# A hybrid decoder step: the four strip products of a group of cached pages placed side by side in TensorE's queue

## Chip, cores and metric

The kernel runs on one core of a Trainium2 chip. The metric is the device time of one launch in microseconds, as the median of several runs. The trace is of one execution of the same program.

## The reference

One decoder layer is computed for a prompt of 1024 tokens and for 8 sample tokens, each of which has 4096 cached positions in 32 pages of 128. What matters here is the attention of the sample tokens over their pages:

```python
past_k = cache_k[l][page_table].reshape(dec_batch, -1, 2 * DA_HEADS, DA_HEAD_DIM)
past_v = cache_v[l][page_table].reshape(dec_batch, -1, DA_HEADS, DA_VDIM)
...
s = jnp.einsum('bqnd,bknd->bnqk', qf, k.astype(jnp.float32)) * DA_SCALE
scores.append(jnp.where(rel >= 0, s - slopes * rel, NEG_INF))
...
p = jax.nn.softmax(jnp.concatenate(scores, axis=-1), axis=-1)
p = p.reshape(B, DA_HEADS, 2, Lq, p.shape[-1])
a = p[:, :, 0] - lam * p[:, :, 1]
outs.append(jnp.einsum('bhqk,bkhv->bqhv', a[..., start:start + n], v.astype(jnp.float32)))
```

Around it stand, for the prompt and the sample tokens alike, a gated feed-forward network (1024 to 2816 and back), one input projection, a linear recurrence with four heads, the attention with four heads of two maps each, one output projection, and a second feed-forward network.

## The kernel before, in words

**The main stream** is the dense work: the feed-forward networks (L382 for the gate and up products, L441 for the down products), the input projection (L508) and the output projection (L382 again). Every product is done in three parts with operands split into a high and a low half (`wH`, `wL`, `xn`, `h`). Weights come as 256 KB tiles `wr` by a DMA that SyncE issues (L360); ScalarE makes `wH` of them and VectorE or GpSimd `wL` (L110).

**Side streams** are woven into it. One does the recurrence and the attention of the prompt (L666 to L862). The other, the sample stream, goes through the pages of the 8 sample tokens. For token b it loads the 32 key pages into tiles `kv` (L984), multiplies each by the query on GpSimd (L1014) and sums on VectorE into the scores `sS` (L1015). After token b's last key page come its softmax (L1023 to L1049) and then, while the key pages of token b+1 pass, its value pages. Key and value pages share 8 buffers `kv`.

**The value pages are taken in groups of four** (`VP = 4`), 64 groups in all. When the fourth page of a group has been asked for, four *strip products* (L1065) multiply the group's 32 columns of weights (128 x 32) with the four pages (128 x 512), one page each, into rows 0 to 31, 32 to 63, 64 to 95 and 96 to 127 of one PSUM tile `mx`: strip j stands in columns 32j to 32j+31 of the array. VectorE then adds the tile to `sacc` (L1069, or L1067 for the first group of a token). There are 256 strip products; the trace shows each as two MATMUL records (two passes over the same 512 columns), so 512 records. `mx` has two buffers, which the recurrence (L690, L691) and the attention's scores (L821) use as well.

**What sets the order**: the program is written out in one order, and a list scheduler with a timeline of its own gives each engine its queue. An instruction's rank is its place in the written order, less an offset where a block is marked: `hp(n)` moves what is in it up by n instructions, and `tc.issue_after(x)` holds what is in it until x has been placed. Most evacuations of the main stream stand in `hp()` (6000), the prompt's side stream in `hp(3000)`, the sample stream in none. Each engine then works through its queue in order, and waits on semaphores.

Of the kernel before, what the change touches and what calls it, by code (L numbers as in the profile page):

```python
# [63 lines left out]
def kernel(ctx: ExitStack, tc: tile.TileContext, I, O):  # L64
    nc = tc.nc
    ACT, DVE, POOL, PE, SP = nc.scalar, nc.vector, nc.gpsimd, nc.tensor, nc.sync
# [12 lines left out]
    def ST(tag, shape, dt=F32, bufs=1):  # L79
        return samp.tile(shape, dt, name=tag, tag=tag, bufs=bufs)  # L80
# [7 lines left out]
    def MX():  # L88
        return psum.tile([P, 512], F32, name="mx", tag="mx", bufs=2)
# [10 lines left out]
    def hp(n=6000):  # L100
        return tc.high_priority(offset=n)
# [875 lines left out]
    def page(name, src, i):  # L977
        t = kv()
        if i % 4 == 0:

            with tc.issue_after(issued[-4].ins) if len(issued) >= 4 else nullcontext():
                _, numbers[name] = nc.values_load_multi_w_load_instructions(pages[0:1, i:i + 4], engines=[SP.engine], min_val=0, max_val=NPOOL - 1,
                                                                             skip_runtime_bounds_check_because="the page table holds numbers of pages")
        issued.append(SP.dma_start(t, src[bass.ds(numbers[name][i % 4], 1)].rearrange("o t c -> (o t) c")))  # L984
        return t

    def sample_attention():
# [65 lines left out]
        vts = {}  # L1053

        def values(b, i):
            Sb = S[b][0]
            vts[i % VP] = page("v", cv, b * NPG + i)
            if i % VP < VP - 1:
                return
            if i == VP - 1:  # L1060
                S["acc"] = ST("sacc", [P, 512], bufs=1)
            po = MX()
            w = Sb.rearrange("p i n -> p (i n)")[:, 8 * (i - VP + 1):8 * (i + 1)]
            for j in range(VP):
                PE.matmul(po[32 * j:32 * j + 32, :], w, vts[j], start=True, stop=True, tile_position=(0, 32 * j))  # L1065
            if i == VP - 1:
                DVE.tensor_copy(S["acc"], po)  # L1067
            else:
                DVE.tensor_tensor(out=S["acc"], in0=po, in1=S["acc"], op=ALU.add)  # L1069

        VP = 4
# [7 lines left out]
        for b in range(NB + 1):  # L1079
            if b < NB:  # L1080
                begin(b)
            for i in range(NPG):
                if b < NB:
                    keys(b, i)
                    yield 1.2
                if b > 0:
                    values(b - 1, i)
                    yield 1.2
            if b > 0:
                end(b - 1)  # L1090
            if b < NB:
                softmax(b)
# [240 lines left out]
```

## Time and profile before

| what | value |
|---|---|
| median of 3 runs | 2511.26 us (2506.85 to 2513.51) |
| the profiled execution | 2503.05 us |
| its span, first to last instruction | 2501.2 us |
| TensorE busy in the span | 2433.6 us (97%) |
| VectorE, ScalarE, GpSimd busy | 1592.6, 924.7, 797.9 us |

The profiled execution's own time lies 1.85 us above its span and 8.21 us below the median of the runs. "Busy" counts the time in which an engine executes at least one instruction; matmuls overlap, so their starts, not their durations, tell what one costs.

### The profile page before, as it was taken

Reading aid. Unit: us, or ns where it says so; the run is one execution under the profiler, and the core shown is the slowest. Engines: PE = TensorE matmul, PEld = TensorE weight load, DVE = VectorE, ACT = ScalarE, POOL = GpSimd, SP = SyncE. Lnnn points to the kernel's source line nnn. Section 1 sums busy time; section 2 is a strip of 40 time slices with the busy share of each in tenths; the row PEclk is TensorE's granted clock in tenths of the full one; section 3 lists DMA queues with packets and bytes.
Section 4 is the critical chain, followed back from the end, with each engine's and each line's share of the span. In section 5 each row is a group of like instructions: output and inputs, shape, how many; then the busy total and the mean of one; then the engine's idle time right before and its main releaser. Section 6 shows DMA issues by size and latency. Waiting matters only on the chain.

```text
span 2501.2 us, 44071 instructions
## 1 busy us (share of the span) xinstructions
PE 2433.6 (97%) x15613; PEld 2071.6 (83%) x15613; DVE 1592.6 (64%) x3326; ACT 924.7 (37%) x1921; POOL 797.9 (32%) x660
## 2 busy tenths in 40 slices
PE   7999999989999999999999999999999999999999
PEld 6999999979867766777778866767677879999999
DVE  6555656595687655757548678776675765655554
ACT  4332334435433322434444433323344544322222
POOL 4100001380243434544435454554452220000000
PEclk9999999999999999999999999999999999999999
DMA  4333334684465647667666775566676743233332
GB/s 135 91 92 93 100 93 119 199 287 128 136 198 165 191 152 214 214 194 237 195 202 187 229 241 156 178 203 188 209 226 189 203 141 117 89 91 92 94 94 73
DMA packets 273534, 402.35 MB, mean 161 GB/s; under 512 B 29785, under 2 KB 104794, under 8 KB 273314
## 3 DMA queue, kind: packets, MB, share of 16 engines
q1 hardware_dynamic: 273314, 399.54, 52.4%
q8 instruction: 123, 2.02, 0.3%
q14 instruction: 97, 0.79, 0.1%
HBM read 361.23 MB, written 38.21 MB: 160 GB/s over the span
## 4 chain that ended last, share of the span: by engine, by line
PE 64%; DVE 6%; DMA 4%; POOL 2%; issue 1%; ACT 1%; SPq 1%; POOLq 0%; DVEq 0%; ACTq 0%
PE mm L382 31%; PE mm L441 13%; PE mm L508 6%; PE mx L1065 6%; DMA kv<-in_cache_k 2%; PE my L723 1%; PE mx L821 1%; POOL kv L1014 1%; PE my L851 1%; DMA xt<-ot 1%; DVE sS L1015 1%; DVE wL L110 1%; PE mx L690 0%; PE my L844 0%; PE mx L691 0%
## 5 line engine op out<-in xcount | busy, mean ns | idle before, releaser
L382 PE MATMUL mm<-xn,wH 128*128 128x256 f32 (+2 forms) x4800 | 1110.5, 324 | 6.0 <-DVE ft L482 2.5
L382 PEld LDWEIGHTS mm<-xn,wH 128*128 128x128 f32 x4800 | 795.4, 190 | 113.4 <-issue 42.8
L382 PE MATMUL mm<-xn,wL 128*128 128x256 f32 (+2 forms) x2400 | 777.0, 324 | 0.0
L110 ACT CAST wH<-wr 128x512 fp32r<-128x512 f32 x672 | 413.6, 619 | 826.8 <-PE mm L382 433.0
L110 DVE TENSOR_TENSOR wL<-wr,wH 128x512 fp32r<-128x512 f32 x504 | 410.5, 816 | 195.1 <-ACT wH L110 157.0
L382 PEld LDWEIGHTS mm<-xn,wL 128*128 128x128 f32 x2400 | 454.6, 189 | 55.0 <-issue 19.3
L441 PE MATMUL mm<-h,wH 128*128 128x264 f32 (+2 forms) x2112 | 489.1, 324 | 5.6 <-DVE tiny L701 2.8
L1014 POOL TENSOR_TENSOR kv<-kv,ss 128x512 f32<-128x512 f32 x256 | 357.9, 1404 | 426.8 <-DMA kv<-in_cache_k 299.1
L441 PEld LDWEIGHTS mm<-h,wH 128*128 128x128 f32 x2112 | 348.3, 189 | 58.5 <-issue 21.8
L441 PE MATMUL mm<-h,wL 128*128 128x264 f32 (+2 forms) x1056 | 340.4, 322 | 0.0
L508 PE MATMUL mm<-wH,xn 128*128 128x256 f32 (+1 forms) x1728 | 325.9, 288 | 7.7 <-DVE ft L482 3.9
L110 POOL TENSOR_TENSOR wL<-wr,wH 128x512 fp32r<-128x512 f32 x168 | 228.5, 1361 | 270.2 <-ACT wH L110 224.1
L421 POOL TENSOR_TENSOR ft<-ft,acc 128x256 f32<-128x256 f32 (+1 forms) x110 | 101.8, 926 | 666.1 <-DVE ft L419 663.5
L508 PEld LDWEIGHTS mm<-wH,xn 128*128 128x128 f32 (+1 forms) x1728 | 260.1, 181 | 28.6 <-issue 14.2
L1015 DVE TENSOR_REDUCE sS<-kv 128x8 f32<-128x512 f32 x256 | 172.4, 679 | 137.5 <-POOL kv L1014 137.1
L508 PE MATMUL mm<-wL,xn 128*128 128x256 f32 (+1 forms) x864 | 248.0, 287 | 1.3 <-POOL wL L110 0.9
L441 PEld LDWEIGHTS mm<-h,wL 128*128 128x128 f32 x1056 | 199.3, 189 | 21.3 <-issue 7.5
L443 DVE SCALAR_TENSOR_TENSOR xr<-mm,xr 128x264 f32<-128x264 f32 (+2 forms) x288 | 146.2, 512 | 104.9 <-PE mm L441 104.3
L1065 PE MATMUL mx<-kv,sS 128*32 128x512 f32 x512 | 165.4, 604 | 0.2 <-DVE sS L1049 0.2
L508 PEld LDWEIGHTS mm<-wL,xn 128*128 128x128 f32 (+1 forms) x864 | 156.1, 181 | 9.6 <-issue 5.0
L419 DVE TENSOR_TENSOR ft<-ft,mm 128x256 f32<-128x256 f32 (+2 forms) x132 | 67.2, 509 | 77.5 <-PE mm L382 77.2
L110 ACT CAST h<-ft 128x256 fp32r<-128x256 f32 (+2 forms) x132 | 63.1, 478 | 92.6 <-POOL ft L421 76.5
(219 smaller groups left out, 2299.2 us busy)
## 6 DMA issues: line engine op xcount, KB each, us to landing
kv<-in_cache_k SPq DMA_DIRECT2D x256, 256.0 KB
kv<-in_cache_v SPq DMA_DIRECT2D x256, 256.0 KB
wr<-in_ffn_w_gate SPq DMA_DIRECT2D x176, 256.0 KB
wr<-in_ffn_w_up SPq DMA_DIRECT2D x176, 256.0 KB
wr<-in_ffn_w_down SPq DMA_DIRECT2D x176, 256.0 KB
wr<-in_w_in SPq DMA_DIRECT2D x96, 256.0 KB
aq<-qt SPq DMA_DIRECT2D x64, 128.0 KB
wr<-in_w_out SPq DMA_DIRECT2D x32, 256.0 KB
```

Source lines behind the costliest of these rows:

```text
L110: return ACT.copy(H, src), (eng or DVE).tensor_tensor(out=L, in0=src, in1=H.bitcast(F32), op=ALU.subtract)
L382: newest[0] = PE.matmul(ps[:, :w], a, b[k][:, :w], start=k == 0 and j == 0, stop=k == n - 1 and j == 2)
L419: DVE.tensor_tensor(out=t, in0=t, in1=pu[:, :sl.w], op=ALU.mult)
L421: POOL.tensor_tensor(out=t, in0=t, in1=sl.acc, op=ALU.mult)
L441: newest[0] = PE.matmul(ps[:, :w], a[:, cs], b[:, :w], start=j == 0 and q == 0, stop=j == m - 1 and q == 2)
L443: DVE.scalar_tensor_tensor(out=sl.xr[d][:, :w], in0=ps[:, :w], scalar=0.25, in1=sl.xr[d][:, :w], op0=ALU.mult, op1=ALU.add)
L508: newest[0] = PE.matmul(ps[:tb, 0:256], a, b, start=k == 0 and j == 0, stop=k == KC - 1 and j == 2)
L723: PE.matmul(pa[:, i * 64:i * 64 + 64], XL[:, i], right(XR[:, i], l0 + i), start=True, stop=True)
L821: PE.matmul(ps[:, :m], qx[:, j, x], KT[:, j, pc * 512:pc * 512 + m], start=x == 0, stop=x == 1)
L1014: POOL.tensor_tensor(out=kt, in0=kt, in1=qb, op=ALU.mult)
L1015: DVE.tensor_reduce(out=Sb[:, i], in_=kt.rearrange("p (n d) -> p n d", d=64), op=ALU.add, axis=AX.X)
L1065: PE.matmul(po[32 * j:32 * j + 32, :], w, vts[j], start=True, stop=True, tile_position=(0, 32 * j))
```

## The change

The four strip products of a group are written so that the newest page's comes first, in a block that is moved up by 5000, and the other three are held until it has been placed.

```diff
             po = MX()
             w = Sb.rearrange("p i n -> p (i n)")[:, 8 * (i - VP + 1):8 * (i + 1)]
-            for j in range(VP):
-                PE.matmul(po[32 * j:32 * j + 32, :], w, vts[j], start=True, stop=True, tile_position=(0, 32 * j))
+
+            def strip(j):
+                return PE.matmul(po[32 * j:32 * j + 32, :], w, vts[j], start=True, stop=True, tile_position=(0, 32 * j))
+
+
+            with hp(5000):
+                m = strip(VP - 1)
+                with tc.issue_after(m.ins):
+                    for j in range(VP - 1):
+                        strip(j)
             if i == VP - 1:
                 DVE.tensor_copy(S["acc"], po)
```

In TensorE's queue of before, the 256 strip products stand in 156 pieces (a piece is a stretch of strip products with nothing else between them): 121 pieces of one, 13 of three, 20 of four and 2 of eight (two groups). After the change there are 62: 60 of four and 2 of eight. As a group is placed as a whole, it also stands earlier among the main stream's products: by 19 instructions that are no strip products in the median of the 64 groups, at most by 86.

The first group in TensorE's queue, before (`mx_8517` is the group's PSUM tile, `kv_8238` to `kv_8514` its pages, `mm_8917` a tile of the main stream):

```order
L382 MATMUL mm_8917<-xn_7987,wH_8833 128x512
L1065 MATMUL mx_8517<-kv_8238,sS_6262 32x512
L666 MATMUL mx_8694<-hgL_8182,sufr_6693 128x512
L667 MATMUL mx_8694<-hgH_8181,sufr_6693 128x512
L1065 MATMUL mx_8517<-kv_8330,sS_6262 32x512
L1065 MATMUL mx_8517<-kv_8417,sS_6262 32x512
L1065 MATMUL mx_8517<-kv_8514,sS_6262 32x512
L382 MATMUL mm_8917<-xn_7986,wL_8834 128x512
```

The same place in TensorE's queue after the change:

```order
L382 MATMUL mm_8917<-xn_7987,wH_8833 128x512
L1066 MATMUL mx_8517<-kv_8514,sS_6262 32x512
L1066 MATMUL mx_8517<-kv_8238,sS_6262 32x512
L1066 MATMUL mx_8517<-kv_8330,sS_6262 32x512
L1066 MATMUL mx_8517<-kv_8417,sS_6262 32x512
L666 MATMUL mx_8694<-hgL_8182,sufr_6693 128x512
L667 MATMUL mx_8694<-hgH_8181,sufr_6693 128x512
L382 MATMUL mm_8917<-xn_7986,wL_8834 128x512
```

Here the newest page's strip leads and the two products of the recurrence come behind the four. The fifth group (`mx_9485`) in TensorE's queue, before:

```order
L382 MATMUL mm_9466<-xn_7975,wH_9446 128x512
L1065 MATMUL mx_9485<-kv_9359,sS_6262 32x512
L382 MATMUL mm_9466<-xn_7974,wL_9447 128x512
L1065 MATMUL mx_9485<-kv_9410,sS_6262 32x512
L382 MATMUL mm_9466<-xn_7980,wH_9446 128x512
L1065 MATMUL mx_9485<-kv_9437,sS_6262 32x512
L382 MATMUL mm_9466<-xn_7981,wH_9446 128x512
L1065 MATMUL mx_9485<-kv_9483,sS_6262 32x512
L382 MATMUL mm_9466<-xn_7980,wL_9447 128x512
```

And after:

```order
L382 MATMUL mm_9397<-xn_7957,wH_9332 128x512
L1066 MATMUL mx_9485<-kv_9483,sS_6262 32x512
L1066 MATMUL mx_9485<-kv_9359,sS_6262 32x512
L1066 MATMUL mx_9485<-kv_9410,sS_6262 32x512
L1066 MATMUL mx_9485<-kv_9437,sS_6262 32x512
L382 MATMUL mm_9397<-xn_7956,wL_9333 128x512
```

Four pieces with one main product between them became one piece; it stands in the main stream's tile `mm_9397`, 44 instructions ahead of where its first strip stood. In SyncE's queue the newest page of this group (`kv_9483`) is asked for, before, here:

```order
L360 DMA wr_9611<-in_ffn1_w_up 128x512
L984 ISA
L984 DMA kv_9479<-in_cache_k 128x512
L360 DMA wr_9617<-in_ffn1_w_up 128x512
L984 ISA
L984 DMA kv_9483<-in_cache_v 128x512
```

And after:

```order
L360 DMA wr_9605<-in_ffn1_w_gate 128x512
L984 ISA
L984 DMA kv_9479<-in_cache_k 128x512
L360 DMA wr_9611<-in_ffn1_w_up 128x512
L984 ISA
L984 DMA kv_9483<-in_cache_v 128x512
```

The page moved up in SyncE's queue by one weight tile. For the group `mx_11474`, whose strips moved up by 85 instructions, the newest page stands behind the same weight tile as before.

## Rows read from the trace of the kernel before

**Rows 1.** The page's first lines: span, and busy time of each engine.

```profile
span 2501.2 us, 44071 instructions
...
PE 2433.6 (97%) x15613; PEld 2071.6 (83%) x15613; DVE 1592.6 (64%) x3326; ACT 924.7 (37%) x1921; POOL 797.9 (32%) x660
```

**Rows 2.** Stages: length, busy PE, PEld, DVE, ACT, POOL; clock, DMA share, GB/s.

```profile
680.00:1200.00 520.00, 512.15 (x2325) 369.25 (x2325) 342.99 (x717) 181.76 (x388) 224.15 (x175) 0.99 0.64 196
...
sum 1266.00, PE 1239.46 PEld 918.78 DVE 853.12 ACT 467.32 POOL 572.55; mean PE 413.15 PEld 306.26 DVE 284.37 ACT 155.77 POOL 190.85
```

**Rows 3.** TensorE's waits, 680 to 1946 us: total, times, longest.

```profile
PE my L723 <- DVE hE L697: 4.9, 1, 4.9
...
PE mx L1065 <- DVE sS L1049: 0.2, 1, 0.2
```

**Rows 4.** The page's group of the strip products.

```profile
L1065 PE MATMUL mx<-kv,sS 128*32 128x512 f32 x512 | 165.4, 604 | 0.2 <-DVE sS L1049 0.2
```

**Rows 5.** Timeline of TensorE, a lone strip and its neighbour: start, us.

```profile
739.97 1.04 PE L1065 MATMUL mx<-kv,sS 128*32 128x512 f32 x2
740.95 0.50 PE L382 MATMUL mm<-xn,wL 128*128 128x512 f32 x1
741.37 1.05 PE L1065 MATMUL mx<-kv,sS 128*32 128x512 f32 x2
```

**Rows 6.** Timeline of TensorE, a group of four in one piece.

```profile
1826.11 0.63 PE L382 MATMUL mm<-xn,wH 128*128 128x512 f32 x2
1826.66 1.06 PE L1065 MATMUL mx<-kv,sS 128*32 128x512 f32 x8
1827.66 0.50 PE L382 MATMUL mm<-xn,wL 128*128 128x512 f32 x1
1828.00 0.63 PE L382 MATMUL mm<-xn,wH 128*128 128x512 f32 x2
1828.46 0.40 PE L382 MATMUL mm<-xn,wL 128*128 128x512 f32 x1
```

**Rows 7.** Timeline of TensorE, a piece of three strips.

```profile
680.58 0.40 PE L667 MATMUL mx<-hgH,sufr 128*128 128x512 f32 x1
680.91 1.06 PE L1065 MATMUL mx<-kv,sS 128*32 128x512 f32 x6
681.89 0.50 PE L382 MATMUL mm<-xn,wL 128*128 128x512 f32 x1
682.23 0.63 PE L382 MATMUL mm<-xn,wH 128*128 128x512 f32 x2
```

**Rows 8.** Timeline of TensorE's weight loads, a group of four in one piece.

```profile
693.47 0.16 PEld L1065 LDWEIGHTS mx<-kv,sS 128*32 128x32 f32 x8 [0.37 <-ACT wH L110]
```

**Rows 9.** Timeline of SyncE: newest value pages of three groups are asked for.

```profile
726.59 0.33 SPq L984 DMA_DIRECT2D kv<-in_cache_v  x1
...
928.49 0.34 SPq L984 DMA_DIRECT2D kv<-in_cache_v  x1
...
1622.90 0.33 SPq L984 DMA_DIRECT2D kv<-in_cache_v  x1
```

**Rows 10.** Timeline of TensorE: strips of the second and third of these groups.

```profile
952.54 1.05 PE L1065 MATMUL mx<-kv,sS 128*32 128x512 f32 x2
...
1628.02 1.06 PE L1065 MATMUL mx<-kv,sS 128*32 128x512 f32 x8
```

**Rows 11.** Waits of GpSimd and ScalarE, 680 to 1946 us: total, times, longest.

```profile
POOL kv L1014 <- DMA kv<-in_cache_k: 274.7, 107, 7.6
ACT wH L110 <- PE mm L382: 199.0, 91, 7.5
POOL wL L110 <- ACT wH L110: 170.8, 63, 10.3
...
POOL tiny L204 <- DVE tiny L203: 41.8, 19, 4.0
...
POOL ft L421 <- DVE ft L419: 20.7, 10, 3.7
```

## Prediction

> **What bounds the kernel now.** I read the page's busy times first. TensorE is busy for 2433.6 of 2501.2 us, and no other engine passes 64% [rows 1]: the end moves when TensorE has less to do or waits more. The strip products all lie between 680 and 1946 us, so I asked for the stages of that stretch next. There TensorE is busy for 1239.5 of 1266 us, VectorE for 853.1 (67%), GpSimd for 572.6 (45%), ScalarE for 467.3, and the DMA engines are used to about 0.64 [rows 2]. So 26.5 us are all that TensorE loses to waits in it, the longest single wait of its list is 4.9 us, and the strips themselves waited 0.2 us in total [rows 3]. What shortens TensorE's queue here should shorten the kernel, unless another engine takes over.
>
> The strips take more of that queue than their work asks for. The page gives them 165.4 us of busy time [rows 4], and the timeline shows why: one strip alone, two passes, is busy for 1.04 us [rows 5], and four strips side by side, eight passes, for 1.06 us [rows 6]. Three take 1.06 us as well [rows 7]. The strips of a piece run at the same time, and a piece costs the same whatever it holds. As a check on the count of pieces: 121 x 1.045 + 13 x 1.06 + 20 x 1.06 gives 161.4 us, and the remaining 4 us are two pieces of eight.
>
> **The change part by part.** No instruction is added or removed; what changes is the number of pieces, and where they stand.
>
> *Price of a piece.* Busy time is not the price, since products overlap; starts are. Main products of 512 columns follow each other by 0.23 us (two in 1828.46 - 1828.00 = 0.46) [rows 6].
> - A lone strip between main products: 741.37 - 739.97 = 1.40 us from one strip's start to the next, with one main product between them: 1.40 - 0.23 = 1.17 us [rows 5]. Of this 0.98 is the time until the next product starts (740.95 - 739.97); 0.19 is wider spacing around it.
> - A piece of three: 682.23 - 680.58 = 1.65 us for it and two other products, so 1.65 - 0.46 = 1.19 us [rows 7].
> - A piece of four: 1828.00 - 1826.11 = 1.89 us for it and three main products, so 1.89 - 0.69 = 1.20 us [rows 6].
>
> *The sum on TensorE.* Before: 121 x 1.17 = 141.6, 13 x 1.19 = 15.5, 20 x 1.20 = 24.0, together 181.1 us. After: 60 x 1.20 = 72.0 us. The two pieces of eight stand in both queues and cancel. TensorE's queue gets shorter by 109.1 us. An error of 0.02 us in the price of a lone strip would move this by 2.4 us, so the uncertainty is not here.
>
> *A rule that speaks against it.* Eight weight loads of a four-strip piece occupy 0.16 us together, from 693.47 on, so all of them are over before the first pass ends [rows 8]. The Trainium skill, in "TensorE: Matmul & The Clock Gate", section Part 3 on packing small matmuls, says that a weight load overlaps matmuls in flight only when its row group differs; the four strips use all 128 rows, so by that rule each strip's load would wait for the strip before it. Only the wider spacing would then be saved, 94 fewer pieces x 0.19 = 18 us, and the sum would be 2503 - 18 = 2485 instead of 2394 us. The trace disagrees: by that rule no eight passes could fit into 1.06 us.
>
> *The move up in the queue.* A group now stands 19 instructions earlier in the median, about 4.4 us at 0.23 us each, and its strips wait at the head of an in-order queue if the newest page has not landed; main products, recurrence and attention stand behind them. The trace doesn't show when a value page lands. The nearest row is GpSimd's wait for key pages, of the same size and from the same queue: 274.7 us in 107 waits, 2.57 us each, 7.6 at most [rows 11]. Bounds: nothing (a group that stood 1628.02 - 1622.90 = 5.1 us behind its page's issue started without idle time [rows 9, 10]), and 2.57 us for every one of the 62 groups in the stretch, 159 us. I went through the groups with the shift of their strips and of their page: two come near. The group `mx_9485` started 739.97 - 726.59 = 13.4 us after its page was asked for [rows 5, 9]; 44 instructions earlier is 10.1 us less, so 3.3 us. The group `mx_11474` had 952.54 - 928.49 = 24.0 us [rows 9, 10] and moves up by 85, 19.6 us, so 4.5 us. For the other 60 the page's request moves up too, or the lead stays above 5 us. I take two waits of 2.57 us, 5 us in all.
>
> *What was hidden and gets less cover.* The other engines must do the same work in a stretch of about 1157 us instead of 1266. VectorE's share goes from 67 to 853.1 / 1157 = 74%, GpSimd's from 45 to 49%, the DMA share from 0.64 to about 0.70. The weights have cover: ScalarE waited 199.0 us for TensorE to give back weight tiles in the L382 products alone [rows 11], so casts run ahead. For VectorE's and ScalarE's chains being late a little more often I add a fifth of the 26.5 us of waits, 5 us. VectorE's own waits for strips only get shorter, which costs and gains nothing.
>
> *Sum.* 2503.05 - 109.1 + 5 + 5 = 2403.9 us for an execution like the profiled one. The median of the runs lies 8.2 us above it (2511.26 - 2503.05), so 2412 us for a median.
>
> **The rivals.**
> - *GpSimd's page chain becomes the bound and takes back half.* In the stretch GpSimd is busy for 572.6 us and waits 274.7 + 170.8 + 41.8 + 20.7 = 508 us for others than TensorE [rows 2, 11]; that makes 1081 us, 76 under the 1157 expected. If the denser stretch lengthens those waits by a quarter, 127 us, the stretch lasts 1208 us, 58 are saved and the time is 2453 us. For it speaks that pages and weights share SyncE's queue; against it, that ScalarE, on which a third of these waits hangs (170.8 us), itself waits 199.0 us for TensorE, and this wait shrinks first.
> - *The strips wait for their newest page: slower.* Moved up, each group blocks TensorE until its page lands. At 109.1 / 62 = 1.76 us per group the gain is gone; at 2.57 us each it is 159 - 109 = 50 us slower, 2561 us. For it: the block is moved ahead of the main stream's ready products. Against it: the leads above, of which two in 62 fall below 5 us.
> - *The weight loads of neighbouring strips queue up*, each behind the strip before it. A piece of four then costs 4 x 0.98 + 0.19 = 4.11 us where four lone strips cost 4.68; each of the 156 - 62 = 94 pieces fewer saves its 0.19 us of spacing and no more, 18 us, and the time is 2493 us. Against it stand the pieces of four in this very trace, at 1.20 us [rows 6, 8]. It is the rule of the skill cited above.
> - *Nothing reaches the end*: the whole 109 us comes back as waits of TensorE on VectorE and ScalarE, 2511 us. This takes five times the 26.5 us of waits that it has in the stretch now.
>
> **How the numbers follow.** The forecast, 2386 to 2430 us, has a chance of 0.76; half taken back 0.12; slower through page waits 0.05; queueing loads 0.02; nothing 0.05. The low end is the sum without new waits (2394 + 8 = 2402), with 12 us of the old ones gone and the spread of the runs (the lowest is 4.4 under the median) taken together, 2386. Half taken back stands for all between 2430 and 2500, with its middle at 2453; the high end goes there, which leaves out the last three cases and about half of that one, so 2386 to 2455 holds about 0.8. The measurement tells about 0.3% from no change, 7.5 us: faster 0.90, the same 0.05, slower 0.05.
>
> **What would show it.** The strips' busy time on the page falls from 165.4 to 60 x 1.06 + 4 = 68 us, and every timeline row of them says x8 or x16. TensorE's busy time falls by close to 100 us and the stretch of the strips by about the same. Idle time in front of the strips stays under 10 us, most of it at the groups `mx_9485` and `mx_11474`; the list of TensorE's waits in the stretch stays near 30 to 40 us. I would be wrong if strips wait for value pages in many groups, if GpSimd's waits for key pages grow while TensorE's waits on VectorE and ScalarE do, or if four strips that wait for four different pages don't start together.

## The result

The changed kernel takes 2451.03 us in the median of 4 runs (2447.88 to 2457.49), the kernel before 2510.62 in the median of 4. The ratio is 0.977, with an interval from 0.974 to 0.979: faster by 59.6 us between the medians, by 52 to 65 us by the interval. The time is 39 us above the forecast of 2412 and outside the forecast proper, 2386 to 2430 us, which had a chance of 0.76. It lies in the case "half taken back", which had 0.12, and close to the 2453 us of that rival. It is inside the range up to 2455 only because the high end of that range was put into this case.

The first lines of the page after the change, to be held against [rows 1]:

```profile
span 2455.7 us, 44078 instructions
...
PE 2342.3 (95%) x15613; PEld 2064.1 (84%) x15613; DVE 1577.9 (64%) x3326; ACT 918.6 (37%) x1921; POOL 795.8 (32%) x660
```

TensorE is busy for 91.3 us less, while the span fell by 45.5 us only. Its idle time in the span, the difference of the two numbers, went from 67.6 to 113.4 us. The profiled execution (2457.49 us) is the longest of the four.

The strip products, as a group of the stretch from 680 to 1900 us, and one piece in the timeline of TensorE, to be held against [rows 4, 6]:

```profile
L1066 PE MATMUL mx<-kv,sS 128*32 128x512 f32 x512 | 69.2, 616 | 6.7 <-DMA kv<-in_cache_v 3.6 <-DVE atn L823 1.5 <-DVE sS L1049 1.1
```

```profile
731.05 0.63 PE L382 MATMUL mm<-xn,wH 128*128 128x512 f32 x2
731.61 1.06 PE L1066 MATMUL mx<-kv,sS 128*32 128x512 f32 x8
732.61 0.50 PE L382 MATMUL mm<-xn,wL 128*128 128x512 f32 x1
732.94 0.62 PE L382 MATMUL mm<-xn,wH 128*128 128x512 f32 x2
```

The strips' busy time is 69.2 us where 68 were forecast. The piece costs 732.94 - 731.05 = 1.89 us with three main products, 1.20 us by itself, as in [rows 6]. So the part of the sum that is about pieces held.

What did not hold is in the stages (columns as in [rows 2]) and in TensorE's waits of the stretch:

```profile
680.00:1200.00 520.00, 495.55 (x2520) 387.47 (x2519) 359.93 (x748) 190.66 (x419) 239.79 (x185) 0.99 0.68 209
1200.00:1440.00 240.00, 219.18 (x1533) 194.63 (x1531) 160.52 (x347) 102.93 (x214) 111.00 (x87) 0.95 0.70 217
1440.00:1900.00 460.00, 433.09 (x2159) 327.82 (x2158) 322.58 (x676) 168.52 (x333) 217.75 (x165) 0.99 0.64 198
sum 1220.00, PE 1147.83 PEld 909.92 DVE 843.03 ACT 462.11 POOL 568.54; mean PE 382.61 PEld 303.31 DVE 281.01 ACT 154.04 POOL 189.51
```

```profile
PE my L723 <- DVE hE L697: 6.0, 2, 4.1
PE my L739 <- DVE hAT L732: 5.9, 4, 2.5
PE my L862 <- DVE aos L858: 5.4, 3, 2.6
PE my L862 <- DVE atn L827: 4.5, 2, 3.8
PE mm L441 <- DVE xr L443: 4.2, 5, 1.7
PE nm L285 <- DVE dg L284: 3.9, 1, 3.9
PE mx L1066 <- DMA kv<-in_cache_v: 3.6, 3, 1.7
```

The strips now end before 1900 us instead of before 1946. In that stretch TensorE is idle for 1220 - 1147.8 = 72.2 us; it was 26.5 [rows 2]. No single wait is large, but of all of TensorE's waits there, 71.7 us by this list, 61.1 us are for VectorE; before, it was 20.9 of 26.6. Behind VectorE stands the chain of the key pages. These are the longest waits of the other engines in the stretch, to be held against [rows 11], and VectorE's wait at the key reduces as it was before, 680 to 1946 us:

```profile
POOL kv L1014 <- DMA kv<-in_cache_k: 316.0, 125, 9.5
DVE sS L1015 <- POOL kv L1014: 202.5, 119, 4.6
ACT ap L828 <- DVE atn L827: 125.1, 42, 6.6
POOL wL L110 <- ACT wH L110: 124.1, 43, 6.8
ACT wH L110 <- PE mm L382: 113.6, 66, 4.3
```

```profile
DVE sS L1015 <- POOL kv L1014: 132.3, 90, 5.8
```

ScalarE's wait for TensorE to give back weight tiles, the cover of the forecast, went from 199.0 to 113.6 us. VectorE's wait at the key reduces rose by 70 us. How much of it TensorE feels can be followed in the two traces: for each wait of TensorE for VectorE, go back through VectorE's unbroken work to the last wait that VectorE itself had. That was a key reduce waiting for GpSimd's multiply for 42.1 of the 61.1 us after the change, and for 7.4 of the 20.9 us before it.

One such wait, in the timelines of VectorE, TensorE and GpSimd:

```profile
856.70 1.29 POOL L1014 TENSOR_TENSOR kv<-kv,ss 128x512 f32<-128x512 f32 x1 [3.81 <-DMA kv<-in_cache_k]
```

```profile
858.03 0.69 DVE L1015 TENSOR_REDUCE sS<-kv 128x8 f32<-128x512 f32 x1 [3.99 <-POOL kv L1014]
858.63 0.68 DVE L1077 TENSOR_TENSOR sacc<-mx,sacc 128x512 f32<-128x512 f32 x1
859.23 0.55 DVE L696 TENSOR_TENSOR hXR<-hE,hqt 128x384 f32<-128x384 f32 x1
...
861.00 1.61 DVE L697 TENSOR_TENSOR hE<-hE,hkT 128x384 f32<-128x384 f32 x1
```

```profile
860.37 0.39 PE L382 MATMUL mm<-xn,wH 128*128 128x512 f32 x1
862.66 0.88 PE L723 MATMUL my<-hXR,hE 128*128 128x64 f32 x6 [1.90 <-DVE hE L697]
```

A key page lands late; GpSimd waits 3.81 us for it; VectorE's queue stands 3.99 us at the reduce of that page; behind the reduce stand the products of the recurrence that TensorE needs, and TensorE waits 1.90 us. Only one of these instructions has to do with the strips, VectorE's addition of a strip tile (L1077, 0.68 us), and it isn't what VectorE waited for.

### The profile page after: what moved, and what is told of

It reads as the page before. It is cut to its first block, busy times and chain, and to the rows that moved or that the text cites. A ratio compares the mean times of both kernels' runs of the same rounds, so it can differ in the third digit from the quotient of the medians.

```text
span 2455.7 us, 44078 instructions
## 1 busy us (share of the span) xinstructions
PE 2342.3 (95%) x15613; PEld 2064.1 (84%) x15613; DVE 1577.9 (64%) x3326; ACT 918.6 (37%) x1921; POOL 795.8 (32%) x660
## 3 DMA queue, kind: packets, MB, share of 16 engines
q1 hardware_dynamic: 273314, 399.54, 53.6%
## 4 chain that ended last, share of the span: by engine, by line
PE 54%; DMA 8%; DVE 8%; POOL 3%; issue 3%; ACT 1%; SPq 1%; POOLq 0%; ACTq 0%; DVEq 0%
PE mm L382 27%; PE mm L441 11%; PE mm L508 6%; DMA kv<-in_cache_k 5%; POOL kv L1014 2%; PE mx L1066 2%; PE my L723 1%; DVE sS L1015 1%; PE mx L821 1%; DVE wL L110 1%; PE my L851 1%; DMA xt<-ot 1%; DMA kv<-in_cache_v 1%; DVE hXR L696 1%; PE my L844 1%
## 5 line engine op out<-in xcount | busy, mean ns | idle before, releaser
L441 PE MATMUL mm<-h,wH 128*128 128x264 f32 (+2 forms) x2112 | 483.5, 322 | 11.4 <-DVE xr L443 7.3
L441 PEld LDWEIGHTS mm<-h,wL 128*128 128x128 f32 x1056 | 199.0, 188 | 16.1 <-issue 1.7
L419 DVE TENSOR_TENSOR ft<-ft,mm 128x256 f32<-128x256 f32 (+2 forms) x132 | 67.1, 508 | 61.5 <-PE mm L382 61.1
L828 ACT ACTIVATE ap<-ap,atn 128x128 f32<-128x128 f32 (+7 forms) x64 | 49.7, 776 | 139.8 <-DVE atn L827 131.1
```

The source lines that it names most:

```text
L419: DVE.tensor_tensor(out=t, in0=t, in1=pu[:, :sl.w], op=ALU.mult)
L441: newest[0] = PE.matmul(ps[:, :w], a[:, cs], b[:, :w], start=j == 0 and q == 0, stop=j == m - 1 and q == 2)
L828: ACT.activation(sb[:, :n], sb[:, :n], AF.Exp, bias=tn[:, 4 + j:5 + j], accum_out=tn[:, 6 + j:7 + j])
```

## The experiments

Ratios are to the kernel before, timed in the same runs; its medians there were 2506.2, 2505.9 and 2504.8 us. By its ratio of 0.977 the changed kernel would take about 2448 us in these.

**Side by side, but not moved up** (`e1_side_by_side_not_moved`):

```diff
-            with hp(5000):
-                m = strip(VP - 1)
-                with tc.issue_after(m.ins):
-                    for j in range(VP - 1):
-                        strip(j)
+            m = strip(VP - 1)
+            with hp(5000), tc.issue_after(m.ins):
+                for j in range(VP - 1):
+                    strip(j)
```

> The newest page's strip keeps its own rank, as in the kernel before; only the other three are drawn up behind it. 63 pieces (62 of four, one of eight), and the groups stand where they stood before the change (median shift 0, -10 to 22). If the stretch's other engines give the gain back (GpSimd's page chain and VectorE's queue behind it), the time stays near the changed kernel's, 2445 to 2458 us, and TensorE's waits between 680 and 1900 us stay near 70 us. If it is the move up in the queue that costs, most of the missing 40 us come back: 2410 to 2425 us, and TensorE's waits in the stretch fall to some 30 us.

Measured: 2467.42 us, ratio 0.985 (0.982 to 0.987). TensorE's idle time between 680 and 1900 us is 1220 - 1145.4 = 74.6 us, VectorE's wait at the key reduces 204.4 us:

```profile
680.00:1900.00 1220.00, 1145.43 (x6151) 907.58 (x6150) 850.15 (x1745) 455.86 (x953) 573.62 (x436) 0.98 0.66 204
```

For 93 pieces fewer, 109 us by their price, the kernel gains 38 us: more comes back here than in the changed kernel, although the groups keep their place. So the move up is not what costs; the kernel without it is slower than the changed one. That extra loss was in neither expectation, whose slowest time was 2458 us. The granted clock was lower in all four runs (0.981 to 0.985, against 0.987 to 0.990 in the changed kernel), which is some 12 us of it as an estimate; the rest stays unexplained.

**Moved up only** (`e12_moved_up_only`), the other half of the change:

```diff
             with hp(5000):
-                m = strip(VP - 1)
-                with tc.issue_after(m.ins):
-                    for j in range(VP - 1):
-                        strip(j)
+                for j in range(VP):
+                    strip(j)
```

> Half of the change: the four strips are moved up by 5000, in the written order, with nothing held behind the newest page's. 71 pieces (59 of four, 2 of three, 9 of one, one of five), 9 more than the changed kernel, 10 us more on TensorE by the price of a piece. If TensorE's queue sets the time there, the ratio is 0.979 to 0.983; if the other engines' chains set most of it, the 10 us are hidden in part and the ratio is 0.974 to 0.979.

Measured: 2446.12 us, ratio 0.978 (0.975 to 0.980), the same as the changed kernel within the intervals. The 9 pieces more were paid for by fewer waits: TensorE is idle for 1220 - 1168.7 = 51.3 us in the stretch, against 72.2.

```profile
680.00:1900.00 1220.00, 1168.73 (x6288) 925.35 (x6287) 863.79 (x1802) 470.59 (x981) 581.30 (x441) 0.98 0.67 209
```

Two orders of nearly the same work thus differ by some 20 us of idle time; `e1_side_by_side_not_moved`, with one piece more than the changed kernel, differs from it by 0.008 of the time, also 20 us. An effect of that size in a single run can't be told from the order of the queues.

**Ten page buffers, after and before** (`e2_ten_buffers_after`, `e3_ten_buffers_before`):

```diff
-    NKV = 8
+    NKV = 10
```

> The changed kernel with ten buffers for key and value pages in place of eight; 63 pieces. If the page chain limits the stretch (a key page is asked for when a buffer comes free, lands some 3 us later, is multiplied for 1.4 us, reduced for 0.7 us, and VectorE's queue stands meanwhile), more buffers ask earlier: VectorE's wait for GpSimd's multiply falls from 202 us to under 130, TensorE's waits in the stretch to 30 to 45 us, and the time to 2410 to 2430 us. If the order of the queues is what costs, or VectorE's load itself, the time stays within 8 us of the changed kernel's 2451.

> The kernel before with ten buffers for the pages; 158 pieces. The control for the run with ten buffers after the change: where TensorE has no time to spare (26 us of waits in the stretch), more buffers can give back at most a part of these waits. Both theories: 2495 to 2512 us. If it falls by 30 us or more, the buffers help by something other than the waits.

Measured: 2455.69 us, ratio 0.980 (0.978 to 0.983) after the change, and 2513.37 us, 1.003 (1.002 to 1.004) before. VectorE's wait fell from 202.5 to 175.3 us, TensorE's idle time in the stretch from 72.2 to 62.5 us, and the time did not fall. VectorE's wait was to fall under 130 us if buffers were short; so two more buffers are not the remedy, and as the wait hardly moved, the run doesn't test what the wait costs. The kernel before came out 1 us above the 2495 to 2512 us expected.

**The reduce written later** (`e4_late_reduce`), and with ten buffers (`e8_ten_buffers_late_reduce`):

```diff
-            POOL.tensor_tensor(out=kt, in0=kt, in1=qb, op=ALU.mult)
-            DVE.tensor_reduce(out=Sb[:, i], in_=kt.rearrange("p (n d) -> p n d", d=64), op=ALU.add, axis=AX.X)
+            m = POOL.tensor_tensor(out=kt, in0=kt, in1=qb, op=ALU.mult)
+            with tc.issue_after(m.ins):
+                flush()
+            held.append((Sb, i, kt))
...
+        def flush():
+            while held:
+                Sb, i, kt = held.pop()
+                DVE.tensor_reduce(out=Sb[:, i], in_=kt.rearrange("p (n d) -> p n d", d=64), op=ALU.add, axis=AX.X)
```

> The changed kernel in which VectorE's reduce of a key page is written behind GpSimd's multiply of the next page, so that its queue should not stand in front of a multiply that runs. 62 pieces. If VectorE standing at the reduce is what makes TensorE wait: VectorE's wait for the multiply falls from 202 to under 60 us, and the time falls to 2410 to 2435 us, unless the buffers, held for one page longer, slow the key pages. If TensorE's waits have another cause, the time stays within 8 us of 2451, whatever VectorE waits for.

> The changed kernel with ten page buffers and the reduce of a key page written behind the multiply of the next, together: the longer hold of a page should no longer slow the requests. If the two were in each other's way when tried alone, VectorE's wait for the multiply falls under 120 us and the ratio to 0.965 to 0.972. If neither reaches what makes the multiply late, the ratio stays at 0.976 to 0.982.

Measured: 2454.72 us, 0.981 (0.977 to 0.984), and 2454.97 us, 0.980 (0.977 to 0.982). VectorE still waited 197.6 and 168.8 us at the reduces: the reduce still came too early for its multiply, so the edit did not take away what it was meant to, and it says nothing against the chain.

**VectorE doesn't wait for the multiply, after and before** (`e5_reduce_does_not_wait`, `e6_reduce_does_not_wait_before`):

```diff
-            DVE.tensor_reduce(out=Sb[:, i], in_=kt.rearrange("p (n d) -> p n d", d=64), op=ALU.add, axis=AX.X)
+            DVE.tensor_reduce(out=Sb[:, i], in_=qb.rearrange("p (n d) -> p n d", d=64), op=ALU.add, axis=AX.X)
```

> The changed kernel in which VectorE's reduces read the query tile instead of the multiplied key page: the same instructions and loads, but VectorE no longer waits for GpSimd's multiply, and the key sums are left out of the scores. 63 pieces. If VectorE's queue standing at these reduces (202 us in 119 waits) is what makes TensorE wait, VectorE's wait there goes to nearly nothing, TensorE's waits between 680 and 1900 us fall from 70 to 30 to 45 us, and the ratio to the kernel before falls from 0.977 to 0.962 to 0.970. If the other chains that TensorE waits for (attention and recurrence through ScalarE and VectorE) are late by themselves, the waits stay above 60 us and the ratio at 0.974 to 0.980.

> The same on the kernel before, as a control; its key sums are left out as well. Its strips stand in 147 pieces, 9 fewer than in the kernel before, which is 10 us less on TensorE by the price of a piece. TensorE waits 25 us in the stretch, so both theories give a fall of 10 to 25 us, ratio 0.990 to 0.997. If it falls by much more, the reduces' wait is no matter of the denser stretch.

Measured: 2511.24 us, 1.002 (1.000 to 1.004), and 2571.83 us, 1.026 (1.023 to 1.028). Both became some 60 us slower, which neither theory had expected. VectorE's timeline in the first of them shows part of why:

```profile
458.34 8.40 DVE L1015 TENSOR_REDUCE sS<-ss 128x8 f32<-128x512 f32 x14 [2.14 <-DMA ss<-zs_aq]
466.66 0.41 DVE L576 TENSOR_TENSOR ez<-ez,qr 128x256 f32<-128x256 f32 x1
```

With nothing to wait for but the query, a token's reduces stand in VectorE's queue in heaps, 14 of them in 8.4 us here, and what TensorE needs waits behind them (11.4 us for one `ez` at 484 us). From 450 to 680 us TensorE is busy for 193.6 us there, against 215.0 in the changed kernel, at a granted clock of 0.90 against 0.96; the rest of the 60 us was not traced. The edit took a wait away and put a bunching in its place, so this pair decides nothing about the chain. It does compare the strips before and after on another base: 2571.83 - 2511.24 = 61 us for 147 - 63 = 84 pieces fewer, 98 us by their price. Part of the gain comes back there too.

**Nothing waits for key pages, after and before** (`e7_no_key_page_wait`, `e9_no_key_page_wait_before`):

```diff
-            POOL.tensor_tensor(out=kt, in0=kt, in1=qb, op=ALU.mult)
-            DVE.tensor_reduce(out=Sb[:, i], in_=kt.rearrange("p (n d) -> p n d", d=64), op=ALU.add, axis=AX.X)
+            pr = ST("spr", [P, 512], bufs=1)
+            POOL.tensor_tensor(out=pr, in0=qb, in1=qb, op=ALU.mult)
+            DVE.tensor_reduce(out=Sb[:, i], in_=pr.rearrange("p (n d) -> p n d", d=64), op=ALU.add, axis=AX.X)
```

> The changed kernel in which GpSimd multiplies the query tile by itself into a tile of its own and VectorE reduces that: key pages are loaded as before but nothing waits for them, and the key sums are left out. 63 pieces. If the pages landing late for GpSimd (316 us in 125 waits) is the head of the chain, TensorE's waits fall to 30 to 45 us and the ratio to 0.960 to 0.970, as with the cut one link further on. If GpSimd's own pace (1.4 us for a multiply) is what VectorE waits for, VectorE's wait stays above 120 us and the ratio above 0.972.

> The control for the run in which nothing waits for key pages: the same cut in the kernel before (key sums left out). 159 pieces, 3 more than before, which is 3 us more. If the page chain costs only where TensorE's own queue is short, the ratio is 0.990 to 1.000, since the kernel before has 25 us of waits in the stretch, and the change then is worth 0.965 to 0.972 between the two kernels without the wait. If the cut frees 30 us or more here as well, ratio 0.988 or less, it helps by something else (less work on GpSimd, buffers free earlier), and the page chain is not shown to take the gain back.

Measured: 2411.77 us, ratio 0.962 (0.960 to 0.965), after the change, and 2499.06 us, 0.998 (0.996 to 0.999), before it. The waits at the key reduces and the stretch, after the change and then before it:

```profile
680.00:1900.00 1220.00, 1186.53 (x6505) 953.74 (x6503) 868.60 (x1856) 499.82 (x1038) 516.56 (x423) 0.99 0.70 215
```

```profile
DVE sS L1016 <- POOL spr L1015: 32.3, 40, 3.1
```

```profile
680.00:1946.00 1266.00, 1248.54 (x6238) 927.80 (x6237) 822.62 (x1745) 473.90 (x968) 498.03 (x415) 0.99 0.64 198
```

TensorE's idle time goes from 72.2 to 33.5 us after the change and from 26.5 to 17.5 us before it; over the whole span, where it doesn't matter that the strips end earlier in this run, from 113.4 to 81.0 and from 67.6 to 68.9. Its waits for VectorE in the stretch go from 61.1 to 18.1 us after the change. The same cut is worth 0.015 of the time, 36 us, in the changed kernel, and 0.002, 6 us, in the kernel before. Between the two kernels without the wait the change is worth 1 - 0.962 / 0.998 = 3.6%, 89 us, for 159 - 63 = 96 pieces fewer, 112 us by their price. With the wait it is worth 59 of 109. So waiting for key pages, with what the cut does besides, takes back some 30 us in the changed kernel that it does not take in the kernel before. This is more than the 20 us by which orders differ, though not by much; the 42.1 us followed in the trace of the changed kernel point the same way. The cut does two other things as well: page buffers are free when a page lands, and GpSimd is busy for less (516.6 us in the stretch instead of 568.5). With the control these help the kernel before by 6 us at most; that they help the denser one no more than that was not shown apart.

**Two tries at the chain's earlier links** (`e10_six_weight_buffers`, `e11_product_in_own_tile`). In the first the raw weight tiles got six buffers, in the second the product of a key page a tile of its own:

```diff
-                raw = DT("wr", [P, 512], bufs=4)
+                raw = DT("wr", [P, 512], bufs=6)
...
-            POOL.tensor_tensor(out=kt, in0=kt, in1=qb, op=ALU.mult)
-            DVE.tensor_reduce(out=Sb[:, i], in_=kt.rearrange("p (n d) -> p n d", d=64), op=ALU.add, axis=AX.X)
+            pr = ST("spr", [P, 512], bufs=2)
+            POOL.tensor_tensor(out=pr, in0=kt, in1=qb, op=ALU.mult)
+            DVE.tensor_reduce(out=Sb[:, i], in_=pr.rearrange("p (n d) -> p n d", d=64), op=ALU.add, axis=AX.X)
```

> The changed kernel with six buffers for raw weight tiles in place of four. SyncE's queue stands 206 us at weight requests that wait for such a buffer, and key pages stand behind them. If that makes the pages late, GpSimd's wait for them falls from 316 to under 260 us and the ratio from 0.977 to 0.966 to 0.973. If the page's own buffers and the chain of landing, multiply and reduce set the pace, the ratio stays at 0.975 to 0.982.

> The changed kernel in which GpSimd writes the product of a key page into one of two tiles of its own, so that the page's buffer is free when the multiply ends and not when VectorE has reduced it. 64 pieces of four. If the pages are asked for late because VectorE frees their buffers late (165 us of SyncE's waits), GpSimd's wait for pages falls by 60 us or more and the ratio to 0.966 to 0.973. If the lateness comes from elsewhere, it stays at 0.974 to 0.982, as it did with ten buffers.

Measured: 2461.00 us, 0.983 (0.981 to 0.986), and 2461.23 us, 0.984 (0.981 to 0.986); neither helped. With six weight buffers SyncE stood at weight requests a little longer (218.7 us against 206.1), so the edit didn't do what it was meant to, and GpSimd waited 300.5 us for pages. With the product in its own tile that wait fell by 58 us, to 257.8, close to the 60 us that were to bring a ratio of 0.973 or less, and yet VectorE waited 181.8 us and TensorE was idle for 1220 - 1144.6 = 75.4 us. How long GpSimd waits is not by itself what TensorE pays; how far VectorE's queue stands behind is nearer to it. Which link makes the pages late stays open.

No version with all its sums beat the changed kernel clear of the intervals; the one that was only moved up is level with it.

## Why the prediction came out as it did

The sum for TensorE's queue held; the sum for the kernel did not, and half of the queue's gain came back. That the time still fell inside the widest range is luck: the range reached into a rival's case, and only half of that rival's mechanism was measured.

**The price of a piece and the count of pieces: right.** 109.1 us was worked out for TensorE's queue, and a piece costs 1.20 us after the change as before. TensorE's busy time fell by 91.3 us, where close to 100 was named. Four strips with four different pages ran as eight passes in 1.06 us: the rule of the Trainium skill that the prediction cites ("TensorE: Matmul & The Clock Gate", Part 3), on weight loads of one row group, does not hold for these column strips, and its rival fell.

**The page waits of the strips: right in size, wrong in place.** 5 us were set down for two groups; 3.6 us in three waits were measured, so the size was right by luck. The group `mx_9485` stood 731.61 - 727.96 = 3.7 us behind its newest page's request (3.3 forecast) and did not wait, nor did the other one:

```profile
727.96 0.33 SPq L984 DMA_DIRECT2D kv<-in_cache_v  x1
```

The groups that waited are others; the longest wait, 1.70 us, was of a group whose page had been asked for 1610.95 - 1608.10 = 2.9 us earlier:

```profile
1610.95 1.06 PE L1066 MATMUL mx<-kv,sS 128*32 128x512 f32 x8 [1.70 <-DMA kv<-in_cache_v]
```

```profile
1608.10 0.34 SPq L984 DMA_DIRECT2D kv<-in_cache_v  x1
```

**The cover of the other engines: the term that was mis-sized.** "A fifth of the 26.5 us of waits, 5 us" was to stand for VectorE and ScalarE being late a little more often. Measured: 72.2 - 26.5 = 45.7 us more idle time, of which the strips' own page waits are 3.6. The step behind it was "ScalarE waited 199.0 us for TensorE ..., so casts run ahead". For the weights this wait did shrink and was not used up (113.6 us left). It says nothing of VectorE's queue, whose instructions for TensorE stand behind reduces that wait for GpSimd, and GpSimd for pages. I had these 132.3 us of VectorE's wait in the trace and did not follow who stood behind them. In the kernel before, TensorE reached its products late enough that this seldom showed: 7.4 us of its waits began at a key reduce, 42.1 us after the change. The pair without the key page wait shows 30 of the missing 50 us there. The remaining 20 were not shown; they are of the size by which orders of nearly the same work differ, and the clock below has a part in them. The prediction's own sign of being wrong came true: GpSimd's waits for key pages grew from 274.7 to 316.0 us while TensorE's waits on VectorE did.

**The clock: a term that was missing.** The mean granted clock fell from 0.992 to 0.987. Lost cycles are (1 - 0.987) x 2455.7 = 31.9 us against (1 - 0.992) x 2501.2 = 20.0, so up to 12 us; this is an upper bound, as it counts TensorE's idle time too. In the stages it shows between 1200 and 1440 us, at 0.95 (0.97 in the same stretch before). With this the profiled execution adds up to within 6 us: 109.1 - 45.8 - 11.9 = 51.4 against 45.5; the rest I can't place.

**From the profiled execution to the median: a term with the wrong sign.** 8.2 us were added because the median lay that far above the profiled execution before. After the change the median lies 6.5 us under it (2457.49 - 2451.03). Between the profiled executions the forecast is off by 2457.49 - 2403.9 = 53.6 us and not by 39: the spread of the runs hid 14.7 us of the miss.

**The first rival** gave the right time, 2453 us, by a mechanism that is only half right. GpSimd's four waits that were to grow by a quarter did not: 316.0 + 124.1 for the two large ones after against 274.7 + 170.8, 500 us for all four against 508. With its 568.5 us of work that is 1069 of 1220 us, so by the rival's own count GpSimd was not the bound. The lateness of the pages was right, and it was VectorE, not GpSimd, through which TensorE felt it. The rival that strips wait for their newest page was wrong.

## What to carry to other kernels

In this kernel products in different column strips of the array cost 1.20 us for four that stand next to each other in the queue, and 1.17 us each when a main product stands between them: count the pieces, not the products. When an engine that bounds a stretch is relieved, ask what its own lateness had covered in the queues that feed it: for each wait of a feeding engine, ask what the bounding engine needs that stands behind it in that queue, even when the bounding engine shows no wait for it now. A cut that removes a wait in a scheduled kernel also moves the instruction, so run the same cut on the kernel before as a control.

## What was not expected of the hardware

After a wait of TensorE of 2.62 us, its products run at half the rate until 1237.4 us: 256-column products follow each other by 0.21 us (1235.80 - 1235.59) and then by 0.12 (1237.53 - 1237.41). The granted clock was 1.00, the upper of its two levels (2.4 GHz), before the wait, 0.50, the lower one (1.2 GHz), behind it, and 1.00 again after that.

```profile
1234.49 0.45 PE L862 MATMUL my<-ident,aos 128*128 128x128 f32 x1 [2.62 <-DVE aos L858]
...
1235.59 0.41 PE L508 MATMUL mm<-wL,xn 128*128 128x256 f32 x1
1235.80 0.63 PE L508 MATMUL mm<-wH,xn 128*128 128x256 f32 x2
...
1237.41 0.28 PE L508 MATMUL mm<-wL,xn 128*128 128x256 f32 x1
1237.53 0.40 PE L508 MATMUL mm<-wH,xn 128*128 128x256 f32 x2
```

```profile
1229.00:1231.00 2.00, 2.00 (x20) 2.00 (x19) 0.00 (x0) 0.87 (x2) 0.00 (x0) 1.00 0.66 195
1235.00:1237.00 2.00, 2.00 (x11) 2.00 (x11) 0.00 (x0) 1.33 (x3) 1.08 (x1) 0.50 0.59 204
1238.00:1240.00 2.00, 2.00 (x19) 2.00 (x18) 0.00 (x0) 0.09 (x1) 0.00 (x0) 1.00 0.80 272
```

This wait thus cost about half as much again as it shows, an estimate: 1.3 us behind it, half of the 2.8 us from 1234.6 to 1237.4, beside the 2.6 us of idle time. Not every such wait does: after one of 2.65 us, which ended at 958.55 us, the granted clock was 1.00 for the next 6 us.

```profile
958.60:965.00 6.40, 6.40 (x33) 4.40 (x34) 3.88 (x13) 2.42 (x7) 0.67 (x1) 1.00 1.10 289
```
